# Two load rates in a planner that orders a transformer trunk: 380 GB/s in the first stage and 270 elsewhere, in place of one

## The chip, the cores and the metric

The program runs on one core of a Trainium2 chip. A core has a matrix engine (TensorE, PE in the profile, with its weight loads shown as PEld), a vector engine (VectorE, DVE), a scalar engine (ScalarE, ACT), GpSimd (POOL) and SyncE (SP), which here only issues DMA transfers. Each engine works through its own list of instructions in order, and an instruction that waits holds up all those behind it on the same engine. The metric is the device time of one execution in microseconds. A profiled execution has a span (first to last instruction) and a time of its own.

## The reference

A decoder trunk of two layers on 256 tokens with 1024 features, in float32. Each layer has a token mixer and a squared-ReLU MLP, each followed by a residual LayerNorm:

```python
def reference(x, ...):
    h = x
    for i in range(DEPTH):                      # DEPTH = 2
        if i % 2 == 0:
            mix = moba_attention(h, moba_w_qkv[j], moba_w_o[j], cos, sin)
        else:
            mix = dilated_attention(h, dil_w_qkv[j], dil_w_o[j], cos, sin)
        h = layer_norm(DEEPNORM_ALPHA * h + mix, ln_mix_g[i], ln_mix_b[i])
        h = layer_norm(DEEPNORM_ALPHA * h + sq_relu_mlp(h, mlp_w_in[i], mlp_w_out[i]), ...)
    return h
```

With 256 tokens and blocks of 256 the first mixer is plain causal attention with 16 heads of 64 and rotary positions. The second has 12 heads in three groups with dilations 1, 4 and 16, mixed by their softmax denominators. The MLP is `square(relu(x @ w_in)) @ w_out` with 4096 hidden features.

## The kernel before, in words

**Number format.** Every float32 operand is split in two: `hi` is the operand rounded to the matrix engine's fp32r, `lo` is what is left. A product is three matmuls (hi by hi, hi by lo, lo by hi). For weights ACT writes `whi` and DVE then writes `wlo` (the helper `split`, lines 309 and 314). All matmuls are issued from line 318, transposes from line 608.

**Weights.** 512 KB tiles of 128 by 1024 floats are loaded from HBM by SP into four buffers named `raw`, split into `whi` and `wlo` (ten buffers each), and used once. A `raw` buffer is free for the next load when both halves of the split have been written.

**The first stage.** The class `Stage` holds one of eight slices of the inner dimension: 256 columns of the transposed input and 512 columns of the first query and key weights, 384 KB in all. The eight slices lie in the four `raw` buffers and, so as not to wait, in the buffers `g`, `b` and two `tok`, which are not yet needed. ACT and DVE split each slice; TensorE then runs 12 matmuls of 256 columns on it (four column blocks by three terms), 96 in the stage. After it come the rotary tables, the value weights (`wv`, four tiles for `v-0`), a mask and the identity, then the query and key weights `wqk`, in a fixed order of loads.

**What follows.** `rotate` applies the rotary tables to the projected queries and keys: ACT copies half-partitions (line 537, `ta<-acc`), DVE multiplies and adds (line 513), ACT and DVE split the result. `do_v` computes values for both halves of the tokens (m = 0 in the PSUM tile `tp`, m = 1 in `acc`). Then scores, softmax (DVE line 584, ACT line 594), transposes (line 608) with their copies `pt` (line 616), the output projection, LayerNorm, the MLP, and the same again for layer 1.

**The order of instructions.** It is not the order in which the kernel is written. The class `Plan` collects every operation with its engine, an estimated cost, and what it reads and writes, and `order` makes a list for each engine, which is then emitted as it stands. It does so in two passes.

- The first pass runs the operations in program order, without limits on buffers, and gives each TensorE operation the time at which it could start as its due time. Operations of other engines get due times backwards from those that use them.
- The second pass is a simulation with buffers. On each engine, of the operations that could start first, the one with the earliest due time is taken. ACT never leaves its place open for a later operation that is due sooner; DVE does so in some cases (`PATIENT`). Loads keep their order.

A load in both passes takes a place on one bus: it starts at the later of its issue plus `FETCH` (1.27 us) and the end of the load before it, takes its bytes divided by `RATE`, and its data count as there `LANDED` (1.6 us) after its end. `RATE` is 270e3 bytes per us, that is 270 GB/s. The costs, the latencies and this rate steer the order alone: nothing in the program that runs depends on them otherwise, since waits are on semaphores.

Of the kernel before, what the change touches and what calls it, by code (L numbers as in the profile page):

```python
# [46 lines left out]
LATS = {("DVE", "DVE"): 0.12, ("DVE", "POOL"): 0.2}  # L47
PE_OUT, PE_IN = 0.25, 0.4
PE_COLD = 5.3
ISSUE, FETCH, RATE, LANDED = 0.47, 1.27, 270e3, 1.6  # L50


def latency(p, q):
    if p.eng == "SP":
        return LANDED
    if p.eng == "PE":
        return 0.0 if q.eng == "PE" else PE_OUT
    return PE_IN if q.eng == "PE" else LATS.get((p.eng, q.eng), LAT)

class Buf:
# [20 lines left out]
class Plan:  # L83
# [16 lines left out]
    def op(self, eng, cost, fn, reads=(), writes=(), xfer=0.0, early=0.0, ahead=0.0):  # L100
        o = Op()
        o.n, o.eng, o.cost, o.fn, o.xfer = len(self.ops), eng, cost, fn, xfer
        o.early, o.ahead = early, ahead
        o.preds, o.succs, o.bufs = set(), [], set()
        for group, is_write in ((reads, False), (writes, True)):
            for item in group:
                b, key = item if isinstance(item, tuple) else (item, None)
                o.bufs.add(b)
                for k, st in b.state.items():
                    if key is None or k is None or k == key:  # L110
                        if st[0] is not None:
                            o.preds.add(st[0])
                        if is_write:
                            o.preds.update(st[1])
                st = b.state.setdefault(key, [None, []])
                if is_write:
                    if key is None:
                        b.state = {None: [o, []]}
                    else:
                        st[0], st[1] = o, []  # L120
                else:
                    st[1].append(o)
        o.preds.discard(o)
        for p in o.preds:
            p.succs.append(o)
        for b in o.bufs:
            b.left += 1
        self.ops.append(o)
        return o

    def order(self):
        clock = {e: BEGIN[e] for e in ("PE", "SP")}
        bus = 0.0
        for o in self.ops:
            t = max([clock.get(o.eng, 0.0)] + [p.end + latency(p, o) for p in o.preds])
            o.end = t + o.cost
            if o.eng in clock:
                clock[o.eng] = o.end
            if o.xfer:
                bus = o.end = max(t + FETCH, bus) + o.xfer  # L140
            o.due = t - o.ahead if o.eng == "PE" else None
        t = clock["PE"]
        for o in reversed(self.ops):
            for q in o.succs:
                d = q.due - o.cost - latency(o, q)
                o.due = d if o.due is None else min(o.due, d)
            if o.due is None:
                o.due = t - o.early
        engines = sorted({o.eng for o in self.ops})
        free = {e: BEGIN[e] for e in engines}  # L150
        bus = 0.0
        cand = {e: [] for e in engines}
        slots = {tag: [0.0] * cap for tag, cap in self.caps.items()}
        done = []
        for o in self.ops:
            o.wait = len(o.preds)
            o.ready = 0.0
            if not o.wait:
                cand[o.eng].append(o)

        loads = [o for o in self.ops if o.eng == "SP"]

        def start_of(o):
            s = max(o.ready, free[o.eng])
            need = {}
            for b in o.bufs:
                if not b.held:
                    need.setdefault(b.tag, []).append(b)
            for tag, bs in need.items():
                q = self.queue[tag]  # L170
                spare = 0
                if {id(b) for b in q[: len(bs)]} != {id(b) for b in bs}:
                    if tag not in LOOSE:
                        return None
                    spare = 1
                if len(slots[tag]) < len(bs) + spare:
                    return None
                s = max(s, sorted(slots[tag])[len(bs) - 1])
            return s

        total = len(self.ops)
        while len(done) < total:
            best = None
            for e in engines:
                lst = [(start_of(o), o) for o in cand[e] if e != "SP" or o is loads[0]]
                lst = [x for x in lst if x[0] is not None]
                if not lst:
                    continue
                first = min(s for s, _ in lst)
                s, o = min((x for x in lst if x[0] <= first), key=lambda x: (x[1].due, x[1].n))  # L190
                if e in PATIENT:
                    worst = PATIENT[e]
                    now, ready = s, o
                    for s2, o2 in lst:
                        if now < s2 < now + ready.cost and o2.due < ready.due:
                            waits = max(s2 - o2.due, s2 + o2.cost - ready.due)
                            runs = max(now - ready.due, now + ready.cost - o2.due)
                            if runs - waits > worst:
                                worst, s, o = runs - waits, s2, o2
                if best is None or s < best[0]:  # L200
                    best = (s, o)
            assert best is not None
            s, o = best
            cand[o.eng].remove(o)
            if o.eng == "SP":
                loads.pop(0)
            for b in o.bufs:
                if not b.held:
                    slots[b.tag].remove(min(slots[b.tag]))
                    self.queue[b.tag].remove(b)  # L210
                    b.held = True
            cost = o.cost * 2 if o.eng == "PE" and s < PE_COLD else o.cost
            free[o.eng] = s + cost
            o.end = s + cost
            if o.xfer:
                bus = o.end = max(s + FETCH, bus) + o.xfer
            done.append((s, o.n, o))
            for b in o.bufs:
                b.left -= 1
                b.last = max(getattr(b, "last", 0.0), o.end + (PE_OUT if o.eng == "PE" else LAT))  # L220
                if not b.left:
                    slots[b.tag].append(b.last)
            for q in o.succs:
                q.wait -= 1
                q.ready = max(q.ready, o.end + latency(o, q))
                if not q.wait:
                    cand[q.eng].append(q)
        done.sort(key=lambda x: x[:2])
        return [o for _, _, o in done]
# [19 lines left out]
def tile_trunk(  # L249
# [23 lines left out]
    nc = tc.nc  # L273
    plan = Plan()
    op = plan.op
# [26 lines left out]
        return n / (1920 if fast else 960) + 0.07 + 0.06 * aps  # L302

    def dma(dst, src, reads=(), writes=(), nbytes=0):
        op("SP", ISSUE, lambda: nc.sync.dma_start(dst(), src), reads, writes, xfer=nbytes / RATE)  # L305

    def split(n, src, hi, lo, r, whi, wlo, sbuf=False, hi_eng="ACT"):
        if hi_eng == "ACT":
# [14 lines left out]
    def load_w(src, n=1024):  # L323
        w = W()
        w.raw = mk([P, 1024], F32, "raw", 4)
        w.hi = mk([P, 1024], F32R, "whi", NSLOT)
        w.lo = mk([P, 1024], F32R, "wlo", NSLOT)
        dma(lambda: w.raw.t[:, :n], src[:, :n], (), [(w.raw, 0)], P * n * 4)
        split(
            n, lambda: w.raw.t[:, :n], lambda: w.hi.t[:, :n], lambda: w.lo.t[:, :n],  # L330
            [(w.raw, 0)], [(w.hi, 0)], [(w.lo, 0)], sbuf=True,
        )
        return w
# [3 lines left out]
    class Stage:  # L337
# [27 lines left out]
        def load(self, c0, c1, keys):  # L365
            c = slice(c0, c1)
            dma(
                lambda: self.raw.t[:, c], xw0[self.kt][:, c], (), [(self.raw, i) for i in keys],
                P * (c1 - c0) * 4,
            )  # L370
# [21 lines left out]
    def const(src, shape, nm):  # L392
        t = mk(shape, F32, nm, 1)
        n = 4
        for d in shape:
            n *= d
        dma(lambda: t.t, src, (), [t], n)
        return t
# [710 lines left out]
```

## Time and profile before

| | |
|---|---|
| median of 3 runs | 578.1 us (577.93 to 578.22) |
| the profiled execution | 577.65 us, of which the span is 575.8 us |
| TensorE busy | 562.3 us, 98% of the span |
| DVE, ACT busy | 418.2 us (73%), 313.3 us (54%) |
| read from HBM | 104.01 MB, 182 GB/s over the span |

A busy share is an average over the whole span. TensorE's ends are modelled, so that its idle time is best read from the starts of its instructions. What can be gained or lost is read where TensorE waits: its wait list, and the timeline around each entry.

### The profile page before, as it was taken

How to read it: one execution, taken by the hardware profiler on the slowest of the kernel's cores; microseconds unless marked ns; L12 is line 12 of the kernel's file. 1: busy time of each engine (PE TensorE's matmuls, PEld its weight loads, DVE VectorE, ACT ScalarE, POOL GpSimd, SP SyncE). 2: the span in 40 equal slices, each digit the busy share in tenths (PEclk: the TensorE clock that was granted, in tenths of full speed). 3: DMA queues.
4: the chain of work that ended last, by engine and by line, in shares of the span. 5: the costliest groups of instructions: out<-in, count | busy, mean ns of one | idle time of the engine just before them, and what ended most of it. 6: DMA issues, size and time to landing. Idle time of an engine off the chain costs nothing.

```text
span 575.8 us, 8591 instructions
## 1 busy us (share of the span) xinstructions
PE 562.3 (98%) x3234; PEld 486.3 (84%) x3234; DVE 418.2 (73%) x729; ACT 313.3 (54%) x529; POOL 8.4 (1%) x13
## 2 busy tenths in 40 slices
PE   8999999999999999999999999999999999999994
PEld 7798798788888888888888997878888888888884
DVE  6798879798775675675678698878966756756544
ACT  6797778456554454455434586844754544544400
POOL 0000000010000000000000000000000000000000
PEclk9999999999999999999999999999999999999998
DMA  8666752627786555555525534434777655555101
GB/s 328 214 207 236 254 178 91 210 73 247 264 270 241 202 193 189 185 200 185 182 79 181 217 122 150 152 127 128 271 263 253 208 191 176 193 183 184 36 1 73
DMA packets 30281, 105.61 MB, mean 183 GB/s; under 512 B 3488, under 2 KB 4256, under 8 KB 30240
## 3 DMA queue, kind: packets, MB, share of 16 engines
q1 hardware_dynamic: 30240, 105.07, 52.8%
q8 instruction: 25, 0.41, 0.3%
q14 instruction: 16, 0.13, 0.1%
HBM read 104.01 MB, written 1.05 MB: 182 GB/s over the span
## 4 chain that ended last, share of the span: by engine, by line
PE 94%; ACT 2%; DVE 2%; DMA 1%; issue 1%; SPq 0%; DVEq 0%; ACTq 0%
PE acc L318 54%; PE tp L318 38%; PE tp L608 2%; ACT ta L537 1%; DVE ta L513 1%; DMA raw<-in_xw_dram 1%; ACT whi L309 1%; DVE tok L520 0%; ACT pt L616 0%; ACT xs L309 0%; DVE wlo L314 0%; ACT ta L772 0%; SPq L305 0%; DVE sc L584 0%; DVE klo L520 0%
## 5 line engine op out<-in xcount | busy, mean ns | idle before, releaser
L314 DVE TENSOR_TENSOR wlo<-raw,whi 128x1024 fp32r<-128x1024 f32 (+2 forms) x185 | 221.8, 1205 | 89.4 <-ACT whi L309 88.1
L309 ACT ACTIVATE whi<-raw 128x1024 fp32r<-128x1024 f32 (+2 forms) x184 | 190.6, 1046 | 142.8 <-PE tp L318 70.0
L318 PE MATMUL acc<-whi,ahi 128*128 128x512 f32 (+1 forms) x312 | 119.5, 383 | 0.0
L318 PE MATMUL acc<-wlo,ahi 128*128 128x512 f32 (+1 forms) x312 | 117.3, 380 | 0.0
L318 PE MATMUL tp<-xs,whi 128*128 128x512 f32 x448 | 112.0, 392 | 0.0
L318 PE MATMUL acc<-whi,alo 128*128 128x512 f32 (+1 forms) x312 | 100.7, 379 | 0.0
L318 PEld LDWEIGHTS tp<-xs,whi 128*128 128x128 f32 x448 | 81.1, 189 | 14.9
L318 PEld LDWEIGHTS acc<-whi,ahi 128*128 128x128 f32 x312 | 58.7, 188 | 11.3 <-issue 0.9
L318 PEld LDWEIGHTS acc<-wlo,ahi 128*128 128x128 f32 x312 | 58.7, 188 | 10.4
L318 PE MATMUL acc<-xs,whi 128*128 128x256 f32 x448 | 65.2, 288 | 0.7 <-ACT whi L309 0.7
L318 PEld LDWEIGHTS acc<-whi,alo 128*128 128x128 f32 x312 | 57.1, 188 | 10.4
L318 PEld LDWEIGHTS tp<-xs,wlo 128*128 128x128 f32 x448 | 61.0, 190 | 4.2
L318 PE MATMUL tp<-xs,wlo 128*128 128x256 f32 x448 | 62.6, 283 | 0.0
L318 PEld LDWEIGHTS acc<-xs,whi 128*128 128x128 f32 x448 | 58.7, 192 | 2.7 <-issue 1.1
L309 ACT ACTIVATE ahi<-ta 128x256 fp32r<-128x256 f32 x56 | 22.8, 407 | 27.2 <-DVE ta L520 27.0
L318 PE MATMUL acc<-xs,wlo 128*128 128x256 f32 x224 | 36.2, 285 | 0.0
L318 PEld LDWEIGHTS acc<-xs,wlo 128*128 128x128 f32 x224 | 30.9, 192 | 0.9 <-issue 0.7
L318 PE MATMUL acc<-whi,xs 128*128 128x512 f32 (+1 forms) x112 | 28.7, 363 | 0.0
L537 ACT ACTIVATE ta<-acc 64x512 f32<-64x512 f32 x28 | 16.6, 592 | 20.8 <-DVE ta L513 10.4
L314 DVE TENSOR_TENSOR alo<-ta,ahi 128x256 fp32r<-128x256 f32 x56 | 23.4, 420 | 6.3 <-ACT ahi L309 6.3
L513 DVE TENSOR_TENSOR ta<-tp,ta 128x256 f32<-128x256 f32 x56 | 23.4, 419 | 5.8 <-ACT ta L762 5.8
L318 PE MATMUL tp<-whi,xs 128*128 128x512 f32 x80 | 25.5, 400 | 1.7 <-ACT whi L309 1.0
(85 smaller groups left out, 527.7 us busy)
## 6 DMA issues: line engine op xcount, KB each, us to landing
raw<-in_win_dram SPq DMA_DIRECT2D x64, 512.0 KB, 4.2
raw<-in_wout_dram SPq DMA_DIRECT2D x64, 512.0 KB, 3.8
raw<-in_wqk_dram SPq DMA_DIRECT2D x24, 512.0 KB, 3.7
raw<-in_wo_dram SPq DMA_DIRECT2D x14, 512.0 KB, 3.3
raw<-in_wv_dram SPq DMA_DIRECT2D x8, 512.0 KB, 6.0
g<-in_lng_dram SPq DMA_DIRECT2D x4, 512.0 KB, 4.9
b<-in_lnb_dram SPq DMA_DIRECT2D x4, 512.0 KB, 6.0
raw<-in_wv1a_dram SPq DMA_DIRECT2D x4, 512.0 KB, 3.2
```

What stands on the lines that cost most here:

```text
L309: op("ACT", act(n, sbuf=sbuf), lambda: nc.scalar.activation(hi(), src(), AF.Copy), r, whi)
L314: lambda: nc.vector.tensor_tensor(lo(), src(), f32(hi()), op=ALU.subtract), list(r) + list(whi), wlo,
L318: nc.tensor.matmul(out_ap, lhsT, rhs, start=start, stop=stop)
L513: op("DVE", dve(n) + extra, lambda: nc.vector.tensor_tensor(out_ap(), a(), b(), op=alu), r, w)
L537: lambda h=h: nc.scalar.activation(b.t[64 * h : 64 * h + 64, :], ps.t[64 - 64 * h : 128 - 64 * h, :], AF.Copy),
L608: nc.tensor.transpose(ps.t[:, c : c + P], src(), ident.t)
```

## The change

The planner's constant rate is replaced by two: a load that starts on the planner's bus at 18 us or earlier takes 380 GB/s, a later one 270 GB/s. Both passes use it. No operation is added or removed, and the loads keep their order; the lists of the engines may come out in another order.

```diff
-ISSUE, FETCH, RATE, LANDED = 0.47, 1.27, 270e3, 1.6
+ISSUE, FETCH, LANDED = 0.47, 1.27, 1.6
+
+BURST, RATES = 18.0, (380e3, 270e3)
 ...
+def landed(t, bus, nbytes):
+    t = max(t + FETCH, bus)
+    return t + nbytes / RATES[t > BURST]
 ...
             if o.xfer:
-                bus = o.end = max(t + FETCH, bus) + o.xfer
+                bus = o.end = landed(t, bus, o.xfer)
 ...
             if o.xfer:
-                bus = o.end = max(s + FETCH, bus) + o.xfer
+                bus = o.end = landed(s, bus, o.xfer)
 ...
     def dma(dst, src, reads=(), writes=(), nbytes=0):
-        op("SP", ISSUE, lambda: nc.sync.dma_start(dst(), src), reads, writes, xfer=nbytes / RATE)
+        op("SP", ISSUE, lambda: nc.sync.dma_start(dst(), src), reads, writes, xfer=nbytes)
```

## The prediction

> **What bounds the kernel now.** I read the page first, then TensorE's wait list, then the stretches of the first 35 us, then the timelines of TensorE, ACT and DVE around the one wait that the change can reach.
>
> ```profile
> span 575.8 us, 8591 instructions
> PE 562.3 (98%) x3234; PEld 486.3 (84%) x3234; DVE 418.2 (73%) x729; ACT 313.3 (54%) x529; POOL 8.4 (1%) x13
> PE 94%; ACT 2%; DVE 2%; DMA 1%; issue 1%; SPq 0%; DVEq 0%; ACTq 0%
> ```
>
> TensorE is busy for 98% of the span and is 94% of the chain that ended last. A new order of the same instructions can only remove TensorE's idle time or add to it. Its wait list (who waited for whom, total, times, longest), first for the first 140 us and then for the rest, shows how little there is:
>
> ```profile
> PE tp L318 <- DVE warm L403: 1.2, 1, 1.2
> PE tp L318 <- ACT whi L309: 1.0, 1, 1.0
> PE tp L608 <- ACT pt L616: 0.8, 2, 0.5
> PE acc L318 <- ACT whi L309: 0.7, 1, 0.7
> PE tp L608 <- DVE mx L584: 0.3, 1, 0.3
> PE tp L318 <- ACT xs L309: 0.3, 1, 0.3
> ...
> PE tp L608 <- ACT pt L616: 1.3, 1, 1.3
> PE tp L318 <- ACT xs L309: 0.3, 1, 0.3
> ```
>
> The first 1.2 us is the start. The 1.0 us, the value matmuls waiting for ACT's `whi`, is the entry that matters here. The stretches (length; busy time of PE, PEld, DVE, ACT, POOL; granted clock, DMA share, GB/s):
>
> ```profile
> 5.00:10.00 5.00, 4.29 (x32) 3.73 (x32) 3.30 (x7) 3.71 (x8) 0.00 (x0) 1.00 1.02 399
> 10.00:15.00 5.00, 5.00 (x44) 5.00 (x43) 3.65 (x8) 2.83 (x7) 0.00 (x0) 1.00 1.04 415
> 15.00:20.00 5.00, 3.97 (x28) 3.52 (x27) 2.37 (x3) 2.95 (x4) 0.00 (x0) 1.00 0.39 149
> 25.00:30.00 5.00, 5.00 (x24) 4.14 (x23) 5.00 (x10) 4.43 (x9) 0.00 (x0) 1.00 0.59 206
> 30.00:35.00 5.00, 5.00 (x38) 4.75 (x37) 4.96 (x14) 4.90 (x12) 0.00 (x0) 1.00 0.67 212
> ```
>
> Loads run at 399 to 415 GB/s from 5 to 15 us; the planner believes in 270. From 15 to 20 us all engines have idle time, and from 25 to 35 us DVE is full. The granted clock is 1.00 in all of them.
>
> **Where the belief shows.** The seam between the first stage and the value matmuls, first the loads (issue rows, and from issue to landing for the first and the fourth value tile in the last column), then ACT, DVE and TensorE:
>
> ```profile
> 7.21 3.17 SPq L305 DMA_DIRECT2D raw<-in_wv_dram  x4
> raw<-in_wv_dram SPq DMA_DIRECT2D x1, 512.0 KB, 6.7
> raw<-in_wv_dram SPq DMA_DIRECT2D x1, 512.0 KB, 7.5
> 20.08 11.55 SPq L305 DMA_DIRECT2D raw<-in_wqk_dram  x6
> ...
> 12.50 0.40 ACT L309 ACTIVATE xs<-tok 128x256 fp32r<-128x256 f32 x1
> 17.00 0.59 ACT L537 ACTIVATE ta<-acc 64x512 f32<-64x512 f32 x1 [4.10 <-PE acc L318]
> 17.50 1.04 ACT L309 ACTIVATE whi<-raw 128x1024 fp32r<-128x1024 f32 x1
> 18.56 0.59 ACT L537 ACTIVATE ta<-acc 64x512 f32<-64x512 f32 x1
> ...
> 13.23 0.42 DVE L314 TENSOR_TENSOR xs<-tok,xs 128x256 fp32r<-128x256 f32 x1
> 17.63 1.29 DVE L513 TENSOR_TENSOR ta<-acc,ropet 128x512 f32<-128x512 f32 x2 [3.97 <-ACT ta L537]
> 18.83 1.22 DVE L314 TENSOR_TENSOR wlo<-raw,whi 128x1024 fp32r<-128x1024 f32 x1
> 28.58 0.41 DVE L314 TENSOR_TENSOR qlo<-ta,qhi 128x256 fp32r<-128x256 f32 x1
> ...
> 17.04 0.40 PE L318 MATMUL acc<-xs,whi 128*128 128x256 f32 x2
> 17.28 0.28 PE L318 MATMUL acc<-xs,wlo 128*128 128x256 f32 x1
> 18.59 1.21 PE L318 MATMUL tp<-whi,xs 128*128 128x512 f32 x4 [1.03 <-ACT whi L309]
> 25.45 1.98 PE L318 MATMUL tp<-wlo,xs 128*128 128x512 f32 x8
> 27.27 1.07 PE L318 MATMUL acc<-whi,xs 128*128 128x512 f32 x4
> 29.99 0.39 PE L318 MATMUL tp<-khi,qhi 128*128 128x512 f32 x1
> 31.02 0.40 PE L318 MATMUL tp<-khi,qhi 128*128 128x512 f32 x1
> ```
>
> The first value tile landed at 7.21 + 6.7 = 13.9 us. ACT had ended its last stage split at 12.90 and sat idle for 4.10 us, because the next entry of its list was a rotary copy of a product that TensorE finished only at 17.0. Only behind it, at 17.50, came the split of the tile that had lain there for 3.6 us. TensorE ran out of work at 17.4 and waited for that split until 18.59.
>
> The planner's sums say why. Its bus starts at 0.74 + 1.27 = 2.01 us. The stage has 3.146 MB, the rotary tables 0.262 MB, a value tile 0.524 MB. At 270 GB/s the first value tile ends at 2.01 + 3.932 / 0.270 = 16.6 and counts as landed at 18.2, after the rotary copy's input: the eighth slice counts as landed at 15.3, its last terms can start 1.7 us later by the planner's costs of the two splits, and with the rest of two column blocks and a latency of 0.25 the product is there at about 17.5. So the copy goes first. At 380 it ends at 12.4 and counts as landed at 14.0, the second at 15.3, the third at 16.7, the fourth at 18.1. That is close to the trace: 13.9 for the first, and for the fourth 7.21 + 3.17 - 0.33 (the length of one issue) + 7.5 = 17.6.
>
> **The change part by part.**
>
> *The rate in the planner (both passes) and the move of the division out of the DMA helper.* No instruction appears or goes; SP's list of loads is fixed, so nothing is moved past it. POOL's few instructions stay where LayerNorm puts them. Direct cost: nothing.
>
> *ACT at the seam.* In the new plan the stage is bound by TensorE from its second slice on (first lo term at 7.3, slice done at 8.5, five slices of 1.44, two column blocks of 0.36, a latency of 0.25), so the copy's input comes at about 16.7, and tile one at 14.0. One split and almost surely two (14.0 to 15.0 and 15.3 to 16.4, at the 1.04 us of the row) go ahead of the first rotary copy. The third, at 16.7, is a tie with it. So TensorE has its first `whi` at 13.9 + 1.04 = 14.9, long before 17.4. The wait goes. From start to start it was 18.59 - 17.28 = 1.31 us, of which 0.12 is the matmul itself (two starts in the 0.24 us from 17.04 to 17.28): **1.19 us gained**. What is late next is the second tile's split, 15.1 + 1.04, also early.
>
> *The value matmuls themselves.* They are 48 of 512 columns, and where they run without a break they start 0.2275 us apart (8 of them from 25.45 to 27.27): 10.92 us. They took 29.99 - 18.59 = 11.40. The excess of 0.48 us is TensorE catching up with splits that alternate with rotary copies on ACT. With ACT and DVE ahead by two tiles, all splits lie earlier than their use: the fourth, landed at 17.6 and split by 19.2 even behind one whole copy (0.59 + 1.04), is needed at 17.4 + 3 x 0.91 = 20.1. I take most of it: **0.4 us gained** (between 0 and 0.48).
>
> *The rotary work is moved back.* What is queued behind the splits on ACT and DVE are the rotary copies and multiplies, which start at 17.4 rather than 17.0 at worst and meet a second pair of splits. Who waits are the scores at 29.99 and 31.02. The second rotation ended at 28.58 + 0.41 = 28.99, 2.0 us ahead of its use. With the scores 1.6 us sooner the slack would be 0.4 if DVE gained nothing; but DVE had 3.97 us idle at the seam and now does two `wlo` of 1.22 us in it, a start of 2.44. Cost: nothing, and if that cover were gone, up to 1.2 us.
>
> *The loads of `wqk`.* A `raw` buffer comes free when its `wlo` is written: with the first at about 14.9 + 1.22 = 16.1, the first `wqk` load goes at about 16.2 in place of 20.08, into a stretch with a DMA share of 0.39. Nobody waits for it now; gain or loss nothing, covered by DVE being the later engine.
>
> *The first stage.* Its 96 matmuls of 0.12 us are nearly gapless from 7 us on, and their data are the same. In the plan the second slice is now behind TensorE rather than ahead of it, which can swap two splits at about 6 us, where the 0.7 us wait for `whi` is. TensorE needs both. I take 0, with 0.3 either way.
>
> *All that follows.* The first pass gives due times. With the old rate its value matmuls end at about 33.5 us: the fourth tile's split is ready at 25.4, 0.9 for its hi terms, 1.8 for the lo terms, 5.4 for m = 1. With the new they are bound by TensorE from 17.2 and end at 28.1. From there on TensorE is the bound in that pass, so all later due times move by the same 5.4 us and compare as before. Buffers and engines stand about 1.6 to 2.4 us earlier, though not all alike, so that the order can differ for some tens of microseconds. The trace has no row for that. The nearest are the waits of layer 0: 0.8 + 0.3 us. I take them as unchanged, with 1.1 gained and 1.1 lost as the ends.
>
> **Sum.** 1.19 + 0.4 = 1.6 us off the profiled execution's 577.65, which gives 576.05. That execution lies 0.45 us below the median of 578.1, so the median comes to **576.5 us**, 0.28% faster.
>
> *A rule against it.* The stretches show 399 to 415 GB/s. The Trainium skill (SBUF — State Buffer, "Summary: rules for kernel authors") says to reckon with about 358 GB/s from HBM to SBUF, so that 380 would be too much to believe in. By it, as an estimate, the fourth tile would land at 2.01 + 5.505 / 0.358 + 1.6 = 19.0 us, its split behind one copy would end 0.5 us after its use at 20.1, and the sum would be 1.1 us, or 577.0. The trace disagrees in this stage: that tile landed at 17.6, so I give this 0.01, within the chance of no change.
>
> **The rivals.**
>
> *The waits of layer 0 go too.* DVE is full from 25 to 35 us, and the copies and maxima that TensorE waits for stand behind it. DVE's head start of 2.4 us is larger than TensorE's 1.6, which speaks for it. Against it: these are chains ACT-DVE-ACT that end in one transpose, placed by the plan. 576.5 - 1.1 = 575.4.
>
> *TensorE arrives earlier and waits later.* If the new order spends DVE's head start on rotations only after the splits, the softmax of the first heads comes out when it did, and the 1.6 us come back as waits at the transposes. For it: DVE at 4.96 of 5 us from 30 to 35. Against it: 1.22 x 2 us of its work lie in time that was idle. 578.1, or 577.3 if half comes back.
>
> *Slower, by the order of the transposes.* The 1.3 us entry of layer 1 shows what one transpose costs that stands in TensorE's list ahead of its time. Layer 0 has eight head pairs, three of which wait now, for 1.1 in all. If each of the three came to 1.3, that is 3.9 - 1.1 = 2.8 more, and 578.1 - 1.6 + 2.8 = 579.3. It decides from 1.6 us more on, and shows as slower from 2.8. Against it: the new plan's landing times are nearer to the chip's than the old one's.
>
> *The change does nothing.* The seam's order would have to stay. The new landing of 14.0 is 2.7 us before the copy's input, so I give this no more than 0.02, inside the second rival.
>
> **How the numbers follow.** About 0.2%, 1.16 us, is what a measurement of this kernel can tell from no change. The forecast has a chance of 0.48, its own range being 576.1 to 577.2 (1.19, with 0 to 0.48 and 0.3 either way); 0.03 of it is within 0.2%. The waits going too has 0.15, all of it faster. TensorE waiting later has 0.22, all within 0.2%. The slower order has 0.15, of which 0.13 is beyond 0.2%. The range reaches from 575.0, the second case with the full 0.48 and 0.3, to 579.0, which takes in the third and leaves out most of the fourth. Faster 0.6, same 0.27, slower 0.13.
>
> **What would show it.** In the changed kernel's timeline ACT has `whi<-raw` at about 14 us and no idle of 4 us after 12.9; DVE has `wlo<-raw` at about 15; the 1.0 us entry of TensorE's wait list is gone and the first value matmul starts at 17.4; the value matmuls run m = 0 and then m = 1 rather than in turns of four; the scores start at about 28.4; the first `wqk` load is issued at about 16. I am wrong if the scores start early and the transposes' entries have grown by as much, or if entries appear in layer 1, whose order I take as unchanged.

## The result and the profile after

The changed kernel takes 576.45 us (median of 8, 575.91 to 577.14) against 578.01 for the kernel before on the same chip (median of 8, 577.57 to 579.27): 1.56 us less. The ratio is 0.9973, with a 95% interval of 0.9962 to 0.9984. The profiled execution took 576.27 us, its span is 574.5.

The planner's lists for the two kernels differ only between 6 and 36 us of its time: 63 entries of TensorE stand at another place, 18 of DVE, 20 of ACT, none of SP or POOL. (Line numbers of the changed kernel are 7 higher: 309 is now 316, 318 is 325, 513 is 520, 608 is 615, 616 is 623.)

Of the page after, the span, the engines and the chain:

```profile
span 574.5 us, 8588 instructions
PE 561.4 (98%) x3234; PEld 486.1 (85%) x3234; DVE 418.9 (73%) x729; ACT 313.8 (55%) x529; POOL 8.4 (1%) x13
PE 87%; DMA 4%; ACT 4%; DVE 3%; issue 1%; SPq 0%; DVEq 0%; ACTq 0%
```

TensorE's wait list after, for the first 140 us and for the rest:

```profile
PE tp L615 <- ACT pt L623: 1.3, 2, 1.0
PE tp L325 <- DVE warm L410: 1.2, 1, 1.2
PE acc L325 <- ACT xs L316: 0.6, 1, 0.6
PE tp L615 <- DVE mx L591: 0.3, 1, 0.3
PE tp L325 <- ACT xs L316: 0.3, 1, 0.3
PE acc L325 <- DVE xs L321: 0.3, 1, 0.3
...
PE tp L615 <- ACT pt L623: 1.3, 1, 1.3
PE tp L325 <- ACT xs L316: 0.3, 1, 0.3
```

The 1.0 us wait of the value matmuls for `whi` is gone. The entry for the copy `pt` has grown from 0.8 to 1.3. Selected rows of ACT, DVE, TensorE and SP's loads at the seam:

```profile
13.60 1.06 ACT L316 ACTIVATE whi<-raw 128x1024 fp32r<-128x1024 f32 x1 [1.27 <-DMA raw<-in_wv_dram]
17.35 1.06 ACT L316 ACTIVATE whi<-raw 128x1024 fp32r<-128x1024 f32 x1 [0.18 <-DMA raw<-in_wv_dram]
18.43 1.20 ACT L544 ACTIVATE ta<-acc 64x512 f32<-64x512 f32 x2
...
14.69 4.97 DVE L321 TENSOR_TENSOR wlo<-raw,whi 128x1024 fp32r<-128x1024 f32 x4 [1.61 <-ACT whi L316]
26.70 0.42 DVE L321 TENSOR_TENSOR qlo<-ta,qhi 128x256 fp32r<-128x256 f32 x1
...
17.14 0.28 PE L325 MATMUL acc<-xs,wlo 128*128 128x256 f32 x1
17.26 3.82 PE L325 MATMUL tp<-whi,xs 128*128 128x512 f32 x16
22.73 3.79 PE L325 MATMUL acc<-whi,xs 128*128 128x512 f32 x16
28.16 0.39 PE L325 MATMUL tp<-khi,qhi 128*128 128x512 f32 x1
29.20 0.40 PE L325 MATMUL tp<-khi,qhi 128*128 128x512 f32 x1
...
15.95 13.84 SPq L312 DMA_DIRECT2D raw<-in_wqk_dram  x6
```

ACT now splits each value tile as it lands (13.60 to 18.4, four of them), DVE follows with four `wlo` in a row, and the rotary work comes behind. TensorE goes from the first stage into the values without a gap at 17.26 and runs them through, m = 0 and then m = 1, until the scores at 28.16, which were at 29.99 before: 1.83 us gained at this point. About 0.5 of it is lost again at 47 us, in this one execution: the `pt` wait there was 0.45 us and is now 0.96.

```profile
47.67 0.44 PE L615 MATMUL tp<-ident,sc 128*128 128x128 f32 x2 [0.96 <-ACT pt L623]
```

### The profile page after: what moved, and what is told of

Read it like the earlier page. It is cut to its first block, busy times and chain, and to the rows that moved or that the text cites. A ratio compares the mean times of both kernels' runs of the same rounds, so it can differ in the third digit from the quotient of the medians.

```text
span 574.5 us, 8588 instructions
## 1 busy us (share of the span) xinstructions
PE 561.4 (98%) x3234; PEld 486.1 (85%) x3234; DVE 418.9 (73%) x729; ACT 313.8 (55%) x529; POOL 8.4 (1%) x13
## 4 chain that ended last, share of the span: by engine, by line
PE 87%; DMA 4%; ACT 4%; DVE 3%; issue 1%; SPq 0%; DVEq 0%; ACTq 0%
PE acc L325 49%; PE tp L325 36%; DMA raw<-in_wv_dram 2%; PE tp L615 2%; ACT whi L316 1%; DVE wlo L321 1%; ACT ta L544 1%; DVE ta L520 1%; DMA raw<-in_wqk_dram 1%; DMA raw<-in_xw_dram 1%; ACT sc L601 0%; DVE tok L527 0%; DVE klo L527 0%; ACT pt L623 0%; ACT khi L556 0%
## 5 line engine op out<-in xcount | busy, mean ns | idle before, releaser
L316 ACT ACTIVATE whi<-raw 128x1024 fp32r<-128x1024 f32 (+2 forms) x184 | 191.0, 1047 | 147.8 <-PE tp L325 69.9
L325 PE MATMUL acc<-whi,ahi 128*128 128x512 f32 (+1 forms) x312 | 119.5, 383 | 0.0
L325 PE MATMUL acc<-wlo,ahi 128*128 128x512 f32 (+1 forms) x312 | 117.3, 380 | 0.0
L325 PE MATMUL tp<-xs,whi 128*128 128x512 f32 x448 | 112.0, 392 | 0.0
L325 PE MATMUL acc<-whi,alo 128*128 128x512 f32 (+1 forms) x312 | 100.7, 379 | 0.0
L325 PEld LDWEIGHTS tp<-xs,whi 128*128 128x128 f32 x448 | 81.1, 189 | 14.9
L325 PEld LDWEIGHTS acc<-whi,ahi 128*128 128x128 f32 x312 | 58.7, 188 | 11.3 <-issue 0.9
L325 PEld LDWEIGHTS acc<-wlo,ahi 128*128 128x128 f32 x312 | 58.7, 188 | 10.4
L325 PE MATMUL acc<-xs,whi 128*128 128x256 f32 x448 | 65.1, 287 | 0.9 <-ACT xs L316 0.6
L325 PEld LDWEIGHTS acc<-whi,alo 128*128 128x128 f32 x312 | 57.1, 188 | 10.5
L325 PEld LDWEIGHTS tp<-xs,wlo 128*128 128x128 f32 x448 | 61.0, 190 | 4.2
L325 PE MATMUL tp<-xs,wlo 128*128 128x256 f32 x448 | 62.6, 283 | 0.0
L325 PEld LDWEIGHTS acc<-xs,whi 128*128 128x128 f32 x448 | 58.6, 192 | 3.0 <-ACT xs L316 1.1
L316 ACT ACTIVATE ahi<-ta 128x256 fp32r<-128x256 f32 x56 | 22.8, 407 | 27.6 <-DVE ta L527 27.5
L325 PE MATMUL acc<-xs,wlo 128*128 128x256 f32 x224 | 36.5, 284 | 0.0
L325 PEld LDWEIGHTS acc<-xs,wlo 128*128 128x128 f32 x224 | 31.0, 192 | 0.7 <-issue 0.7
L325 PE MATMUL acc<-whi,xs 128*128 128x512 f32 (+1 forms) x112 | 28.2, 362 | 0.0
L769 ACT ACTIVATE ta<-tp 128x256 f32<-128x256 f32 x56 | 21.0, 375 | 9.3 <-PE tp L325 9.3
L544 ACT ACTIVATE ta<-acc 64x512 f32<-64x512 f32 x28 | 16.6, 593 | 17.4 <-DVE ta L520 11.2
```

Of the source, the lines that this page charges most:

```text
L316: op("ACT", act(n, sbuf=sbuf), lambda: nc.scalar.activation(hi(), src(), AF.Copy), r, whi)
L325: nc.tensor.matmul(out_ap, lhsT, rhs, start=start, stop=stop)
L544: lambda h=h: nc.scalar.activation(b.t[64 * h : 64 * h + 64, :], ps.t[64 - 64 * h : 128 - 64 * h, :], AF.Copy),
L769: op("ACT", act(S), lambda: nc.scalar.activation(u(), ps.t[:, S:], AF.Copy), [ps], uk)
```

## The experiments

All twelve were timed in three batches, each beside the kernel before on the same chip; the ratios compare within a batch.

| kernel | median, us | before, us | ratio | 95% interval |
|---|---|---|---|---|
| new rates, due times alone | 577.79 | 577.83 | 1.0003 | 0.9994 to 1.0012 |
| new rates, second pass alone | 576.21 | 577.83 | 0.9972 | 0.9962 to 0.9981 |
| one split moved by hand | 577.55 | 577.83 | 0.9994 | 0.9985 to 1.0003 |
| four splits moved by hand | 578.79 | 577.85 | 1.0019 | 1.0008 to 1.0029 |
| changed, value matmuls in turns | 576.87 | 577.83 | 0.9984 | 0.9975 to 0.9993 |
| changed, once more | 576.17 | 577.85 | 0.9969 | 0.9958 to 0.9980 |
| changed, one `wlo` as before | 576.23 | 577.85 | 0.9974 | 0.9965 to 0.9983 |
| 358 and 270 | 575.89 | 577.82 | 0.9967 | 0.9955 to 0.9979 |
| 330 throughout | 577.71 | 577.82 | 0.9999 | 0.9991 to 1.0008 |
| **380 throughout** | **574.09** | 577.85 | 0.9932 | 0.9919 to 0.9944 |
| 430 throughout | 577.91 | 577.82 | 1.0000 | 0.9991 to 1.0010 |
| 600 throughout | 587.40 | 577.82 | 1.0167 | 1.0151 to 1.0183 |

### Which pass: due times or readiness

The new rates in the first pass alone:

```diff
-                bus = o.end = landed(s, bus, o.xfer)
+                bus = o.end = max(s + FETCH, bus) + o.xfer / RATES[1]
```

> The new rates in the planner's first pass alone (due times); the second pass, which decides what is ready when, keeps 270 GB/s. The lists differ from the kernel before only at about 7 to 9 us: two splits of the second slice change places and seven matmuls move. Theory of the seam: within 0.3 us of the kernel before, and TensorE's 1.0 us wait for whi is still there. Rival, that the 0.1 to 0.2 us by which the stage ends sooner in the changed kernel and what follows from it carry the gain: 0.5 us or more below the kernel before.

No difference in the time, and the wait stands: in its wait list the entry reads `PE tp L325 <- ACT whi L316: 1.0, 1, 1.0`, the scores start at 30.12. The new rates in the second pass alone:

```diff
-                bus = o.end = landed(t, bus, o.xfer)
+                bus = o.end = max(t + FETCH, bus) + o.xfer / RATES[1]
```

> The new rates in the second pass alone; due times by 270 GB/s. The lists are those of the changed kernel but for the second slice's two splits, a DVE pair and seven matmuls at 6 to 8 us. Theory of the seam: the same as the changed kernel to 0.3 us, 1.3 to 1.8 us below the kernel before, first value matmul at 17.3 to 17.5. Rival, due times matter: less than half of the gain.

1.62 us less than the kernel before: the whole gain. What counts is when the planner holds an operation for ready. Its old list shows why: there the first value tile was due at 18.18 and the rotary copy at 29.99, so that the due times had always been for the tile, but the copy could start at 18.11 and the tile at 18.18, and ACT takes what can start first. The due times only swap two splits of the second slice, which is worth nothing that can be measured.

### How much of the order is needed

The kernel before, with ACT's first value split put ahead of the first rotary copy in the finished list, and nothing else:

```diff
-        return [o for _, _, o in done]
+        seq = [o for _, _, o in done]
+        seq.remove(self.ops[171])
+        seq.insert(seq.index(self.ops[148]), self.ops[171])
+        return seq
```

> The kernel before, its lists untouched but for one instruction of ACT: the split of the first value tile (whi) stands ahead of the first rotary copy in place of behind it. Theory of the seam: TensorE's 1.03 us wait is nearly all of the gain, and one instruction is enough for it. The first value matmul at about 17.4 us (18.59 before), scores at about 28.8 (29.99 before), time 1.0 to 1.3 us below the kernel before. Rival, that the gain comes from due times and an order that fit as a whole: the wait only moves to the second tile, the scores start at 29.5 or later, and the time is within 0.5 us of the kernel before.

The rival was right. ACT's and then TensorE's timeline of this kernel:

```profile
14.00 1.06 ACT L312 ACTIVATE whi<-raw 128x1024 fp32r<-128x1024 f32 x1 [1.02 <-DMA raw<-in_wv_dram]
17.16 0.59 ACT L540 ACTIVATE ta<-acc 64x512 f32<-64x512 f32 x1 [2.10 <-PE acc L321]
18.51 0.59 ACT L540 ACTIVATE ta<-acc 64x512 f32<-64x512 f32 x1 [0.76 <-DVE ta L516]
19.12 1.06 ACT L312 ACTIVATE whi<-raw 128x1024 fp32r<-128x1024 f32 x1
...
17.56 1.09 PE L321 MATMUL tp<-whi,xs 128*128 128x512 f32 x4
20.24 1.19 PE L321 MATMUL tp<-whi,xs 128*128 128x512 f32 x4 [0.68 <-ACT whi L312]
22.54 1.20 PE L321 MATMUL tp<-whi,xs 128*128 128x512 f32 x4 [0.19 <-ACT whi L312]
29.95 0.39 PE L321 MATMUL tp<-khi,qhi 128*128 128x512 f32 x1
```

The value matmuls start at once, at 17.56, run out of tiles at the second one, and the scores start at 29.95, where they were. ACT's two rotary copies are 1.35 us apart, since the second waits 0.76 us for a multiply of DVE, and the second tile's split stands behind both. So all four were moved, in ACT's list alone:

```diff
+        for n in (171, 174, 177, 180):
+            seq.remove(self.ops[n])
+            seq.insert(seq.index(self.ops[148]), self.ops[n])
```

> The kernel before with all four splits of the value tiles ahead of the first rotary copy in ACT's list; DVE's, TensorE's and SP's lists untouched. One split ahead only moved the wait to the second tile. If ACT's order alone carries the gain: value matmuls from 17.4 without a break, scores at 28.4, time 1.2 to 1.6 us below the kernel before. If DVE's part is needed too (its list still has the two rotary multiplies ahead of the first wlo, and now gets them 1 us later): the value matmuls run through, but the second rotation ends at about 29.8, TensorE waits between 28 and 32 us, and the time is 0.3 to 0.9 us below.

Slower than the kernel before, by 0.19%, which neither of the two expectations had. Rows of TensorE and DVE:

```profile
18.52 1.09 PE L322 MATMUL tp<-whi,xs 128*128 128x512 f32 x4
27.51 0.74 PE L322 MATMUL tp<-wlo,xs 128*128 128x512 f32 x2 [1.00 <-DVE wlo L318]
30.86 0.39 PE L322 MATMUL tp<-khi,qhi 128*128 128x512 f32 x1
41.42 0.87 PE L322 MATMUL tp<-pt,v 128*64 128x256 f32 x8 [0.71 <-ACT pt L620]
...
20.42 1.29 DVE L517 TENSOR_TENSOR ta<-acc,ropet 128x512 f32<-128x512 f32 x2 [5.72 <-ACT ta L541]
26.23 1.22 DVE L318 TENSOR_TENSOR wlo<-raw,whi 128x1024 fp32r<-128x1024 f32 x1
```

DVE's list, left as it was, begins with the two rotary multiplies, and they now wait for copies that stand behind four splits: DVE idles 5.72 us where it had idled 3.97. TensorE waits 1.00 us for the fourth `wlo` in place of 1.03 us for the first `whi`, and the values take 30.86 - 18.52 = 12.34 us. (The late start of 18.52 belongs to the first stage of this execution, whose third slice landed only at 8.25 us.) With DVE still late, a wait of 0.71 us for a copy `pt` follows at 41 us, which the kernel before does not have. The gain is not in one wait but in ACT and DVE changing their order together.

### The order of the value matmuls

The changed kernel, with TensorE's value matmuls in the old turns of four:

```diff
+        for n, m in ((201, 186), (202, 186), (203, 188), (204, 188), (205, 190), (206, 190)):
+            self.ops[n].due = self.ops[m].due + 0.001
         engines = sorted({o.eng for o in self.ops})
```

> The changed kernel, but TensorE's value matmuls in the old order, m = 0 and m = 1 in turns of four (due times of six operations lowered); ACT's list differs by one exchange at 26 us. Theory: the 0.5 us by which the value matmuls took less time (11.40 to 10.90 us) came from splits that are there in time, so with the old turns they still take about 10.9, scores at about 28.2, and the time is within 0.2 us of the changed kernel. Rival, that the order m = 0, then m = 1 saved it: scores at 28.6 or later and 0.4 us above the changed kernel.

```profile
17.79 1.55 PE L327 MATMUL tp<-whi,xs 128*128 128x512 f32 x6
28.70 0.39 PE L327 MATMUL tp<-khi,qhi 128*128 128x512 f32 x1
```

In the trace the values take 28.70 - 17.79 = 10.91 us, as in the changed kernel (28.16 - 17.26 = 10.90). So the 0.5 us came from splits that are there in time and not from TensorE's order. The time is another matter. The median is 0.4 us above that of the changed kernel's first runs, as the rival had it, and 0.66 us above the kernel with the new rates in the second pass alone, timed on the same chip; the profiled execution is not above the changed kernel's (576.29 and 576.27), and the intervals overlap. What the turns cost beside the values, if anything, no trace here shows.

### The half microsecond at 47 us

The changed kernel with no edit:

> The changed kernel once more, beside the next three. The one profile of it has a wait of 0.96 us for the copy pt at 47 us, where the kernel before, and the run with the new rates in the second pass alone, whose lists are the same from 9 us on, have 0.45. If that 0.5 us is chance (a load that landed late), this look has 0.4 to 0.5 there and a span of about 574.0. If it belongs to the first stage's order, it stands again. Time 1.4 to 1.7 us below the kernel before.

The second profiled execution of the changed kernel has 0.45 us there again, and a span of 574.0:

```profile
47.23 0.44 PE L615 MATMUL tp<-ident,sc 128*128 128x128 f32 x2 [0.45 <-ACT pt L623]
```

So the 0.96 was the first profiled execution alone. In it the second load of a value tile for the next heads, issued at 34.10, landed 6.6 us later, and ACT waited 0.42 us for it at 40.70. That DVE's new order had held this load back was tried by putting one `wlo` where it had been:

```diff
+        self.ops[310].due = self.ops[228].due - 0.01
         engines = sorted({o.eng for o in self.ops})
```

> The changed kernel, but the DVE split wlo of the fourth wqk tile goes ahead of the softmax's reciprocal at 31.6 us, as in the kernel before, so that the next load of a value tile is issued at about 32.6 in place of 34.10. Theory, that DVE's new order there costs something because it holds a load back: a load that lands earlier, no wait over 0.5 us at 47 us, up to 0.5 us below the changed kernel. Rival, that the wait at 47 us is set by ACT's own order (a whi of 1.04 us ahead of the copy): 0.45 us there as before, the same time to 0.2 us.

The load goes at 33.35 instead of 34.10; the wait is 0.45 us, as in the second profiled execution, and the time is the same (576.23 and 576.17). The theory that the new order costs something there falls. ACT's timeline of the second execution shows what sets the 0.45:

```profile
45.02 0.59 ACT L544 ACTIVATE ta<-acc 64x512 f32<-64x512 f32 x1 [0.76 <-DVE ta L520]
45.64 1.06 ACT L316 ACTIVATE whi<-raw 128x1024 fp32r<-128x1024 f32 x1
46.60 0.58 ACT L623 ACTIVATE pt<-tp 128x512 f32<-128x512 f32 x1
```

Ahead of the copy that TensorE needs stand a rotary copy that waits 0.76 us for DVE, and a split of 1.06 us.

### The rates themselves

358 GB/s in the first stage:

```diff
-BURST, RATES = 18.0, (380e3, 270e3)
+BURST, RATES = 18.0, (358e3, 270e3)
```

> 358 GB/s in the first 18 us and 270 elsewhere: the rate that the Trainium skill (SBUF — State Buffer, Summary: rules for kernel authors) gives for HBM to SBUF. The seam should be as with 380: value matmuls from 17.4 us without a break, and the time within 0.4 us of the changed kernel, 1.2 to 2.0 us below the kernel before. If 380 is needed there, the fourth tile's split is late and the scores start 0.5 us later.

The time is that of the changed kernel (575.89). The value matmuls run through from 17.86, the scores start at 28.77, 10.91 us later, so the seam does not need 380. The equal time does not mean equal orders, though: between 23 and 185 us of the planner's time 152 entries of DVE and 122 of ACT stand at another place than in the changed kernel, and in layer 0 a wait of 0.4 us for `pt` is left of 0.8 + 0.3. 380 GB/s throughout, that is the change without its second half:

```diff
-BURST, RATES = 18.0, (380e3, 270e3)
+BURST, RATES = 1000000000.0, (380e3, 380e3)
```

> 380 GB/s throughout in place of 270 outside the first 18 us. The seam is the same as in the changed kernel; the lists of DVE and ACT differ from 34 us to 419 us. If the low rate elsewhere does nothing, the same as the changed kernel to 0.3 us. If the planner needs it, since loads outside the first stage land 3 to 7 us after their issue, ACT meets splits whose tiles are not there, and new waits of TensorE on whi appear between 40 and 130 us: 0.5 to 2 us slower than the changed kernel.

I had expected the same time or a slower one. It is 2.1 us below the changed kernel's 576.17 on the same chip, and the fastest kernel here. Its seam is the same (first value matmul at 17.43, scores at 28.34). TensorE's wait list for the first 140 us is what differs:

```profile
PE tp L325 <- DVE warm L410: 1.2, 1, 1.2
PE tp L325 <- ACT xs L316: 0.3, 1, 0.3
PE acc L325 <- DVE xs L321: 0.2, 1, 0.2
```

None of the waits for `pt` and `mx` in layer 0 is left. ACT's list at the first of them:

```profile
44.42 0.60 ACT L623 ACTIVATE pt<-tp 128x512 f32<-128x512 f32 x1 [0.29 <-PE tp L615]
45.05 1.20 ACT L544 ACTIVATE ta<-acc 64x512 f32<-64x512 f32 x2
46.27 0.39 ACT L623 ACTIVATE pt<-tp 128x256 f32<-128x256 f32 x1
```

The copy `pt` goes first, the two rotary copies follow each other with no wait in between, and no split stands ahead. By the start of the first LayerNorm's transposes (116.01 us, 117.55 in the second execution of the changed kernel) 1.54 us are gained, and 0.3 more by the end of the matmuls (564.74 and 566.62). Whether this is because 380 is nearer to the truth was asked with three more rates throughout (the same edit with 330e3, 430e3 and 600e3 for both rates).

> 330 GB/s throughout. 380 throughout was 2.1 us below the changed kernel, with TensorE's three waits in layer 0 (0.6, 0.5, 0.5 us) gone. Theory, that a belief nearer to the real landing orders better everywhere (a 512 KB load outside the first stage lands 3.6 to 4.2 us after its issue; the planner reckons 4.8 at 270, 4.5 at 330, 4.3 at 380, 4.1 at 430, 3.7 at 600): part of the way, 0.7 to 1.8 us below the changed kernel, that is 2.3 to 3.4 below the kernel before. Rival, that which waits stand is a chance of the order: anywhere from 0.5 above to 2 below the changed kernel, with no trend over 330, 380, 430 and 600.

> 430 GB/s throughout. Theory of the nearer belief: at least as good as 380, 3.5 to 4.3 us below the kernel before, the three waits of layer 0 at most 0.3 us each. Rival, chance: 1 to 4 us below, with some of the three waits back.

> 600 GB/s throughout, which no load stream here reaches (399 to 415 GB/s in the first stage), though a single load's landing is about right at 3.7 us. Theory of the nearer belief: the first stage and the value tiles are now believed too early, ACT waits for tiles at its splits, but they stay ahead of the rotary copies; 2.5 to 4 us below the kernel before. Rival, chance: no better or worse than 330 and 430 in any regular way.

There is no trend: 0.1 us below the kernel before at 330, 3.8 below at 380, 0.1 above at 430, 9.6 above at 600. The seam is right in all of them (scores at 28.3 to 28.8). What differs is which waits the order leaves in both layers. The entries for `pt` and `mx` at 330 and then at 430 (first 140 us), and the three longest at 600 (the whole span):

```profile
PE tp L325 <- ACT pt L623: 0.6, 1, 0.6
PE tp L615 <- DVE mx L591: 0.4, 2, 0.3
...
PE tp L325 <- ACT pt L623: 1.6, 3, 0.9
```

```profile
PE tp L325 <- ACT qhi L316: 2.9, 1, 2.9
PE tp L325 <- ACT pt L623: 2.8, 3, 2.1
PE tp L615 <- DVE mx L591: 1.9, 1, 1.9
```

The theory of the nearer belief falls. The bounds given for the rival did not hold either: at 330 and 430 the whole gain is gone, and 600 is far worse than both. No regular link between the rate and the waits is left to see once the lists differ beyond the seam; why 380 came out best is open. At 330 layer 0 is as in the changed kernel (the first LayerNorm's transposes at 117.51 and 117.55) and the loss stands in layer 1 (the matmuls end at 567.59 and 566.62); its profiled execution, 576.76, is the fastest of its eleven, so that the rest of its median stands in no trace.

At 600 two things come besides. ACT then has splits in its list whose tiles are not there, and its own wait list (18 to 130 us) has entries that the changed kernel's lacks at this size:

```profile
ACT whi L316 <- DMA raw<-in_wqk_dram: 4.3, 3, 2.1
ACT whi L316 <- DMA raw<-in_wo_dram: 2.7, 3, 1.5
```

And within 1.4 us of the end of each of TensorE's three longest waits (2.1, 1.9 and 2.9 us) its granted clock is half for 3.4 us (length; busy time of PE, PEld, DVE, ACT, POOL; granted clock, DMA share, GB/s):

```profile
41.60:45.00 3.40, 3.40 (x17) 3.40 (x17) 3.37 (x6) 2.54 (x5) 0.00 (x0) 0.50 0.93 357
51.80:55.20 3.40, 3.40 (x14) 2.36 (x14) 3.40 (x10) 3.40 (x14) 0.00 (x0) 0.50 0.01 5
335.10:338.50 3.40, 3.40 (x16) 3.27 (x15) 2.92 (x11) 2.78 (x6) 0.00 (x0) 0.51 0.23 93
```

Half of 3 x 3.4 us is 5.1 us of lost matmul time, an estimate. With the 6.9 us by which TensorE's wait list is longer than in the second execution of the changed kernel (12.2 and 5.3 us) that makes 12.0, near the 11.6 us between the spans (585.6 and 574.0). In the other kernels, whose longest wait is 1.3 us, the granted clock is 1.00 from 20 to 564 us. That the long waits bring the half clock is an inference from these traces; no run tried it by itself.

## Why the prediction was right, point by point

**Direction and size.** 576.5 us was forecast and 576.45 measured; 1.6 us of gain, and 1.56 measured. That the two are so close is luck: the interval leaves 0.9 to 2.2 us, and the two terms came out larger in the trace (1.83 us at the scores).

**The seam, 1.19 us.** The first value matmul came 18.59 - 17.26 = 1.33 us sooner, 0.14 of it because the first stage ended sooner in that execution; in the second one it came at 17.33, which is 1.26. The cause was as described: with the new rates in the second pass ACT splits the tiles where it had idled. One working was off. I had the old plan's copy ready at 17.5 and the tile at 18.2. In the planner's own list the copy is at 18.11 and the tile ready at 18.18. The old order hung on 0.07 us. I had also let one or two splits go ahead, with the third a tie; all four did. For the fourth the working lacked a rule of the planner. In its new simulation ACT was free at 17.67, with the copy's input there at 17.05 and the fourth tile only at 18.10, but the `ta` buffers are given out in order, and the one ahead of the copy's belongs to DVE's multiply, which DVE had put behind its `wlo`.

**The value matmuls, 0.4 us.** 0.50 (11.40 to 10.90 us), just beyond the upper end of 0.48. The run with the old turns shows that it is the splits in time. But the sum treated the two terms as separate gains of ACT's order. The hand-moved splits show that they are not: one split ahead gives back the first term at the second tile (0.68 + 0.19 us of new waits), and ACT's four without DVE's give back all, part of it at the fourth `wlo` and the rest at the copy `pt` at 41 us.

**The rotary work moved back, nothing.** Right. The second rotation ended at 26.70 + 0.42 = 27.12, 2.1 us ahead of its use at 29.20, because DVE did all four `wlo` of the value tiles before it, from 14.69 on, where I had counted on two in its idle time. ACT's first rotary copy came at 18.43, later than the 17.4 that I had as the worst. What that cover is worth shows in the four hand-moved splits, where DVE lacks it: 0.94 us above the kernel before.

**The loads of `wqk`.** First issue at 15.95 (about 16.2 forecast, 20.08 before). ACT, now ahead, waits 0.59 us for it before its split at 20.22, TensorE does not.

**The first stage, 0 with 0.3 either way.** The two splits did swap; the new due times alone changed nothing that can be measured.

**All that follows, unchanged.** Right, and for the reason given. Later due times moved by one amount: a `wlo` that was due at 46.84 in the old plan is due at 41.40, 5.44 us sooner, against the 5.4 worked out. From 36 us on the lists are the same. The waits of layer 0 were 0.8 + 0.3 us in the second profiled execution, as before. The 1.3 + 0.3 of the first did not come again.

**The rivals.** The slower one, by the order of the transposes, did not come with this change, but its mechanism is real: at 430 throughout three waits for `pt` make up 1.6 us in layer 0. The transposes of its first LayerNorm start at 118.35 us (119.29 before, 117.55 in the second execution of the changed kernel), and what is left of the lead goes in layer 1, where the matmuls end at 568.78 (568.43 before). At 600 such waits decide, with the half clock behind them. The case that the waits of layer 0 go too came with 380 throughout and was worth 2.1 us, more than the 1.1 of the wait list.

**The rule against it.** By the rate of the Trainium skill (SBUF — State Buffer, "Summary: rules for kernel authors"), about 358 GB/s, the sum would have been 1.1 us, an estimate. The changed kernel's stage loads at 392 and 399 GB/s (the stretches of 5 to 10 and 10 to 15 us), so the trace disagrees with it here. As the planner's belief 358 does as well: that kernel is 1.93 us below the kernel before, with a seam that runs through and another order behind it.

## What to carry to other kernels

Where a written-out order puts one engine's idle time beside work that has already landed, first ask what the planner believed to be ready at that moment; the readiness it reckons with decided here, and the due times did not. Moving one engine's instructions by hand did not repair this seam: two engines had to change together, and half the repair was worth nothing or was slower than none. And once a constant changes the lists beyond the place it was meant for, time several values of it: from 330 to 430 GB/s a seam that runs through each time came with results 3.8 us apart, and how near the rate was to the measured one did not tell which.

## What the runs showed that I had not expected

The length of the first stage is not the same from one execution to the next. The first value matmul started between 17.25 and 17.87 us in the ten profiled executions of kernels with the new seam, with the third slice (the fourth load) landing between 6.62 and 7.46 us. It matters less than it may seem: with the values started at 17.77, the kernel with one `wlo` as before ended its matmuls at 567.07 us, and the first profiled execution of the changed kernel, started at 17.26, at 567.06, since it lost 0.5 us at 47 us.

ACT's second rotary copy waits 0.76 us for a multiply of DVE when that multiply stands between the two copies in the planner's common list of all engines (17.16 and 18.51 above, and 45.02), and not at all when it stands behind both (45.05, 1.20 us for both). In ACT's own list the copies are neighbours in all these cases. The copies and the multiply read the same product. Which dependency holds the second copy was not tried.
